# Merge gates as block products: seven products per 2 x 2 block instead of eight, in sweeps over pairs of column tiles, with the attention moved beside the branch gates

## The chip, the cores and the metric

The kernel runs on one NeuronCore of a Trainium2 chip. The metric is the device time of one execution in microseconds (us). The kernel before takes 2950.4 us in the median of 3 runs (2949.13 to 2953.23).

Engines in the profile: PE is TensorE (matmuls), PEld its weight loads, DVE VectorE, ACT ScalarE, POOL GpSimd, SP the engine that issues most DMAs. A product reads its operands from SBUF, sums in PSUM (8 banks), and an eviction by ScalarE or VectorE takes the sum out.

## The reference, cut to what matters

One layer of a decoder runs two token mixers on the same normalized input and merges them with gates. 1088 tokens (1024 of a prompt, 64 of 8 short samples), 2048 channels:

```python
h = rms_norm(x, norm_gain) * (1 + scale[:, None]) + shift[:, None]
u_a, z_a, q, k, v, z_b, g_lr, m_a, m_b = jnp.split(h @ w_in, SPLIT_POINTS, axis=-1)
a_y, sa_re, sa_im = s5_branch(u_a, ...)                       # state space
a_out = (a_y * jax.nn.silu(z_a)) @ w_a_out
b_y, s_gla = gla_branch(q, k, v, log_a, s0_gla, ...)          # gated linear attention
b_out = (b_y * jax.nn.silu(z_b)) @ w_b_out
merged = jax.nn.sigmoid(m_a) * a_out + jax.nn.sigmoid(m_b) * b_out
y = x + gate[:, None] * (merged @ w_out)
```

The merge gates m_a and m_b are 2048 columns each of `h @ w_in`, all in float32.

## The kernel before, in words

**Products.** All activations lie with channels on partitions: `h` is 16 tiles (k) of 128 channels x 1088 tokens. A float32 operand is split into a high and a low part, and a product is three passes: high weight x high activation, high x low, low x high (`mm3`, lines 63 to 71). `w_in` has 72 column tiles (j) of 128 columns. `product` (line 73) takes one column tile after the other: `wload` fetches its weights in four quarters of 128 x 512 (`wsplit`, line 46: SP's DMA into `wraw`, ScalarE writes the high part `whi`, VectorE the low part `wlo`; 6 buffers of each, so one tile and a half ahead). Then three chunks of tokens (320, 384, 384), for each 16 k x 3 passes = 48 matmuls into one PSUM bank `mm` of four, and an eviction: `evict_to` copies to DRAM, `evict_silu` multiplies with the sigmoid first.

With `kouter=True` two column tiles run side by side with k outside (`product_k`, line 91): the three sums of the first lie in `mm` banks, those of the second in three of the four `bg` banks that the work beside uses.

**Work beside the products.** `self.steps` is a generator that lays down small pieces of other work; `product` advances it after the k in `self.ticks` and after each chunk, and in the same way `self.gates`. In the stage of the merge gates it is the gated linear attention (`gla_run`, line 733): 20 units, 4 for the samples and 16 for the prompt (4 heads x 4 blocks of 256 tokens). A unit (`gla_unit`, line 756) is a chain over four engines. Head: gate product (L775), absolute value, exponential and logarithm on ScalarE (L778 to L780), difference and scans on VectorE (L784, L790). Seven levels (three for the samples), each: differences (L814), two exponentials (L815, L816), two products (L817, L818), small matmuls (L831, L840), a masked copy (L833). Tail: transposes (L872), copy (L874), matmuls with values and state (L932, L939, L940) and the state's update (L941), square (L945), sum on GpSimd (L946), mean over channels (L949), root (L132) and scaling. A unit's inputs are loaded while the unit before it runs.

**Order.** The program is laid down in this order: S5 beside the first products; tiles 16 to 31 (q, k, v); tiles 40 to 71 (the merge gates, to DRAM as `mas` and `mbs`) with the attention beside, `ticks` (4, 10); tiles 8 to 15 and 32 to 39 (branch gates `zas` and `zbs`) with `ada_gates` (the last columns of the conditioning product) beside; then both branches' outputs (`branch_a`, `merge`) and the output projection (`final`). The framework reorders what is laid down with a simulation of its own when the kernel is built, keeping all dependencies; what comes out is a fixed list for each engine, and each engine runs its list from the front. Buffers rotate: who allocates one waits for the last reader of what it held.

**Slots.** The pool of activations has 32 slots of 128 x 1088; in these stages `h`, in two parts, fills all of them.

## Time and profile before

| | |
|---|---|
| median of 3 runs | 2950.4 us |
| the profiled execution, its span | 2947.8 us |
| TensorE busy in the span | 2890.1 us (98%) |
| VectorE, ScalarE, GpSimd busy | 1344.5, 941.1, 263.4 us |
| granted TensorE clock, mean over the span | 0.994 |
| moved by DMA | 376.59 MB, 128 GB/s in the mean |

The page also has the chain of work that ended last: 67% of it are matmuls, 20% each on lines 69, 70 and 71, the three passes. In the 40 slices of the span TensorE is below nine tenths only in the first and in the last two.

How to read it: times are us from the span's start. A matmul's row shows from its start to its modelled end, and the next one starts before that, so what one costs is the distance of two starts. "Busy" of a group counts overlaps once. DMA share is the mean busy share of the 16 DMA engines. PEclk is the granted TensorE clock as a share of 2.4 GHz.

### The profile page before, as it was taken

The numbers are of one execution on the slowest core, as the hardware profiler recorded it, in microseconds if no ns is written. First come the engines' busy times: TensorE is split into PE (matmuls) and PEld (weight loads), VectorE is DVE, ScalarE is ACT, GpSimd is POOL, SyncE is SP. The second block draws the span as 40 slices with busy tenths as digits, with TensorE's granted clock in tenths as the row PEclk, the third lists the DMA queues.
The fourth block names the chain that finished last, engine by engine and source line by source line (L and its number), as shares of the span: only waits on it lengthen the run. The fifth ranks groups of instructions, "written<-read, shape, count | busy, mean of one in ns | idle before, by whom it ended". The sixth has DMA issues, their size and how long they took to land.

```text
span 2947.8 us, 49487 instructions
## 1 busy us (share of the span) xinstructions
PE 2890.1 (98%) x19584; PEld 2762.2 (94%) x19584; DVE 1344.5 (46%) x3424; ACT 941.1 (32%) x1735; POOL 263.4 (9%) x430
## 2 busy tenths in 40 slices
PE   7999999999999999999999999999999999999988
PEld 3799999999989999999999999999999999899988
DVE  3587778751234444444453111114662233556455
ACT  4222222222234434443443111422232111444434
POOL 0002122210000000000000000301010000203021
PEclk9999999999999999999999999999999999999999
DMA  9634444442232222222223344423274333555455
GB/s 377 242 117 122 120 128 117 128 123 75 85 126 100 84 83 72 85 80 77 81 86 105 98 146 132 115 76 102 97 231 136 112 114 116 191 164 181 145 173 168
DMA packets 221881, 376.59 MB, mean 128 GB/s; under 512 B 35153, under 2 KB 111729, under 8 KB 219473
## 3 DMA queue, kind: packets, MB, share of 16 engines
q1 hardware_dynamic: 159856, 256.26, 26.8%
q0 software_dynamic: 24720, 75.59, 8.4%
q10 hardware_dynamic: 37072, 41.59, 4.1%
q8 instruction: 154, 2.52, 0.3%
q14 instruction: 79, 0.64, 0.1%
HBM read 288.44 MB, written 76.51 MB: 124 GB/s over the span
## 4 chain that ended last, share of the span: by engine, by line
PE 67%; DMA 2%; DVE 1%; ACT 1%; issue 1%; POOL 0%; DVEq 0%; ACTq 0%; POOLq 0%
PE mm L71 20%; PE mm L69 20%; PE mm L70 20%; DMA wraw<-in_w_out_dram 1%; DMA bz<-zbs 1%; PE bg L831 1%; PE bg L69 1%; PE bg L71 1%; PE bg L70 1%; PE bg L201 1%; PE bg L939 0%; PE bg L940 0%; PE bg L932 0%; DMA mx<-mscr 0%; DVE wlo L56 0%
## 5 line engine op out<-in xcount | busy, mean ns | idle before, releaser
L69 PE MATMUL mm<-hh,whi 128*128 128x384 f32 (+1 forms) x3360 | 1101.3, 329 | 4.2 <-ACT hh L264 4.2
L71 PE MATMUL mm<-hh,wlo 128*128 128x384 f32 (+2 forms) x3360 | 1103.0, 329 | 0.0
L70 PE MATMUL mm<-hl,whi 128*128 128x384 f32 (+1 forms) x3360 | 1100.0, 328 | 2.4 <-DVE hl L266 2.4
L56 DVE TENSOR_TENSOR wlo<-wraw,whi 128x512 fp32r<-128x512 f32 x560 | 406.1, 729 | 634.7 <-ACT whi L54 627.2
L69 PEld LDWEIGHTS mm<-hh,whi 128*128 128x128 f32 x3360 | 630.5, 188 | 19.2 <-issue 10.0
L70 PEld LDWEIGHTS mm<-hl,whi 128*128 128x128 f32 x3360 | 630.6, 188 | 10.1 <-DVE hl L266 3.6
L71 PEld LDWEIGHTS mm<-hh,wlo 128*128 128x128 f32 x3360 | 630.5, 188 | 5.5 <-issue 2.8
L54 ACT ACTIVATE whi<-wraw 128x512 fp32r<-128x512 f32 x560 | 351.3, 630 | 771.8 <-PE mm L70 561.6
L69 PE MATMUL mm<-ahi,whi 128*128 128x384 f32 (+3 forms) x1656 | 542.0, 328 | 13.4 <-DVE y L1084 10.4
L71 PE MATMUL mm<-ahi,wlo 128*128 128x384 f32 (+3 forms) x1656 | 542.2, 328 | 2.9 <-DVE wlo L56 2.9
L70 PE MATMUL mm<-alo,whi 128*128 128x384 f32 (+3 forms) x1656 | 541.6, 327 | 0.0
L69 PEld LDWEIGHTS mm<-ahi,whi 128*128 128x128 f32 x1656 | 313.5, 189 | 17.1 <-issue 11.0
L71 PEld LDWEIGHTS mm<-ahi,wlo 128*128 128x128 f32 x1656 | 313.5, 189 | 4.8 <-DVE wlo L56 3.5
L70 PEld LDWEIGHTS mm<-alo,whi 128*128 128x128 f32 x1656 | 313.6, 189 | 1.1
L635 ACT ACTIVATE ev<-mm 128x384 f32<-128x384 f32 (+1 forms) x120 | 55.9, 466 | 237.4 <-PE mm L71 234.4
L1042 DVE TENSOR_TENSOR m<-m,mm 128x384 f32<-128x384 f32 (+1 forms) x96 | 50.5, 529 | 146.9 <-PE mm L71 146.9
L645 DVE TENSOR_TENSOR ev<-ev,mm 128x384 f32<-128x384 f32 (+1 forms) x45 | 23.8, 530 | 181.3 <-ACT ev L644 181.2
L946 POOL TENSOR_TENSOR on<-on 128x256 f32<-128x256 f32 (+1 forms) x20 | 13.1, 653 | 961.3 <-ACT on L945 961.3
L644 ACT ACTIVATE ev<-mm 128x384 f32<-128x384 f32 (+1 forms) x45 | 21.1, 468 | 176.5 <-PE mm L71 176.3
L1040 ACT ACTIVATE m<-m 128x1088 f32<-128x1088 f32 x32 | 35.6, 1113 | 119.3 <-DMA m<-mbs 91.3
L480 POOL DMA_DIRECT2D tm<-kd x128 | 65.0, 516 | 43.0 <-DMA kd<-kk 18.8
L991 POOL DMA_DIRECT2D yt<-y x64 | 34.1, 540 | 380.1 <-ACT m L207 259.6
(334 smaller groups left out, 2580.6 us busy)
## 6 DMA issues: line engine op xcount, KB each, us to landing
wraw<-in_w_in_dram SPq DMA_DIRECT2D x288, 256.0 KB
wraw<-in_w_out_dram SPq DMA_DIRECT2D x192, 256.0 KB
adaraw<-in_w_ada_dram SPq DMA_DIRECT2D x64, 512.0 KB
gateraw<-in_w_ada_dram SPq DMA_DIRECT2D x16, 1024.0 KB
x<-in_xT_dram SPq DMA_DIRECT2D x16, 544.0 KB
m<-mas POOLq DMA_DIRECT2D x16, 544.0 KB, 4.9
m<-mbs POOLq DMA_DIRECT2D x16, 544.0 KB, 5.0
mscr<-m POOLq DMA_DIRECT2D x16, 544.0 KB, 3.1
```

The lines of the kernel that those rows point to most:

```text
L54: nc.scalar.activation(hi, raw, AF.Copy)
L56: nc.vector.tensor_tensor(lo, raw, hi.bitcast(F32), ALU.subtract)
L69: nc.tensor.matmul(ps, hi[:, c], ah[:, sl], start=start, stop=False)
L70: nc.tensor.matmul(ps, hi[:, c], al[:, sl], start=False, stop=False)
L71: nc.tensor.matmul(ps, lo[:, c], ah[:, sl], start=False, stop=stop)
L201: self.nc.tensor.matmul(ps[i:i + 32, :256], self.c32[:, k, :], raw[:, (k - k0) * 256:(k - k0 + 1) * 256], start=k < 4, stop=k >= KT - 4, t ...
L480: nc.gpsimd.dma_start(tm[16 * s:16 * s + 16], kd[0:16, :, 16 * (7 - s):16 * (7 - s) + P])
L635: nc.scalar.activation(e[:, :n], ps[:, :n], AF.Copy, scale=scale)
L831: nc.tensor.matmul(o, gs, blk(gs, w)[:, :, m:w], start=True, stop=True, tile_position=(0, 32 * i))
L991: nc.gpsimd.dma_start(yv[r:r + 16], self.yscr[2 * i + uu][:, g, :].rearrange("(t h) c -> h t c", h=16))
L1040: nc.scalar.activation(st["m"], st["m"], AF.Sigmoid)
L1042: V.tensor_tensor(mm, mm, ps[:, :n], ALU.mult)
```

## The change

**The sums.** The weights of two neighbouring column tiles, halved over k (8 k tiles each), are a 2 x 2 block matrix a11, a12 (first tile), a21, a22 (second). The activations, halved over k and over tokens (2 x 544), are another: b11, b12, b21, b22. The product of two such matrices, eight block products, is made from seven by the scheme of Winograd and Strassen: the blocks are first added and subtracted (s1 to s4 on the left, t1 to t4 on the right), and the seven products are combined afterwards.

**Sweeps.** There are 16 pairs of column tiles, 8 for `mas` and 8 for `mbs`, each 8 a group. A sweep makes one of the seven products for the 8 pairs of a group; `SWEEPS` names left and right block. One product is 8 k x 2 half-width chunks of 272 tokens x 3 passes = 48 matmuls into two PSUM banks; `left` loads, adds, splits the left block (sums s1 and s2 go to DRAM and come back in the next sweep that uses them); the right block's 8 tiles are loaded during the sweep before into the other one of two sets. Partial results stay in 8 tiles (`pts`), finished quarters go to `mas` and `mbs`. All these tiles take the 32 slots that `h` had.

**Operands.** `blocks` writes the seven right blocks to DRAM (`opscr`), in steps beside the products 28 to 31.

**What moves.** The merge gates now come last before the branches. The branch gates (8 to 15, 32 to 39) come right behind 28 to 31, with the attention beside them, advanced after k 2, 6, 9, 13 and each chunk; `ada_gates` follows the attention in one generator (`behind`), which goes on in the sweeps after k 1, 3 and 5 of each product. The PSUM pool of the products is closed and opened anew on either side of the sweeps.

The diff without its changes of comments (a line of "..." marks what is left out):

```diff
+HT = T // 2
+NC = HT // 2
...
     def psum(self, main):
         if main:
-            return self.pmm.tile([P, 512], F32, tag="mm", name="mm")
+            return self.pmm.tile([P, 512], F32, tag="mm", name="mm", bufs=4)
...
+    SWEEPS = (("a11", "11"), ("a12", "21"), ("s1", "t1"), ("s2", "t2"), ("s3", "t3"), ("a22", "t4"), ("s4", "22"))
+
+    def blocks(self, h):
...
+            def split(name, k, v):
+                st = pp.tile([P, T], F32R, tag="st", name="st", bufs=3)
+                nc.scalar.activation(st[:, :HT], v, AF.Copy)
+                V.tensor_tensor(st[:, HT:], v, st[:, :HT].bitcast(F32), ALU.subtract)
+                nc.gpsimd.dma_start(self.opscr[name][k], st.bitcast(F32))
+            for k in range(8):
+                for name, (hi, lo), o in (("11", h[k], 0), ("21", h[8 + k], 0), ("22", h[8 + k], HT)):
+                    nc.gpsimd.dma_start(self.opscr[name][k][:, :HT], hi[:, o:o + HT].bitcast(F32))
+                    nc.gpsimd.dma_start(self.opscr[name][k][:, HT:], lo[:, o:o + HT].bitcast(F32))
+                x, y = (pp.tile([P, T], F32, tag=n, name=n, bufs=2) for n in "xy")
+                yield
+                V.tensor_tensor(x, h[k][0].bitcast(F32), h[k][1].bitcast(F32), ALU.add)
+                V.tensor_tensor(y, h[8 + k][0].bitcast(F32), h[8 + k][1].bitcast(F32), ALU.add)
+                b11, b12, b21, b22 = x[:, :HT], x[:, HT:], y[:, :HT], y[:, HT:]
+                V.tensor_tensor(b11, b12, b11, ALU.subtract)
+                split("t1", k, b11)
+                yield
...
+    def left(self, w, an, pair, q, scr, raws):
...
+        elif an == "s1":
+            x = both(blk(j2, 0), blk(j2, 1), ALU.add)
+            nc.gpsimd.dma_start(scr[0][:, q, :], x)
+        elif an == "s2":
+            x = both(load(scr[0][:, q, :]), blk(j1, 0), ALU.subtract)
+            nc.gpsimd.dma_start(scr[1][:, q, :], x)
...
+        hi = self.wp.tile([P, QK4], F32R, tag="whi", name="whi", bufs=6)
+        nc.scalar.activation(hi, x, AF.Copy)
+        lo = self.wp.tile([P, QK4], F32R, tag="wlo", name="wlo", bufs=6)
+        nc.vector.tensor_tensor(lo, x, hi.bitcast(F32), ALU.subtract)
+        return hi, lo
+
+    def sweeps(self, w, groups):
...
+        ops = [self.act(F32R, "op") for _ in range(16)]
+        sets = [ops[:8], ops[8:]]
+        right = lambda b, k, o: nc.sync.dma_start(o.bitcast(F32), self.opscr[b][k])
+        for k in range(8):
+            right("11", k, sets[0][k])
+        pts = [self.act(F32, "pt") for _ in range(8)]
+        rawt = [self.act(F32, "raw") for _ in range(4)]
+        fint = [self.act(F32, "fin") for _ in range(4)]
...
+                for i, (pair, dst) in enumerate(group):
+                    ps = self.pmm.tile([P, 2, 512], F32, tag="mm2", name="mm", bufs=2)
+                    for q in range(2):
+                        hi, lo = self.left(w, an, pair, q, self.wscr[i], raws)
+                        for k in range(4):
+                            c = slice(k * P, (k + 1) * P)
+                            b = B[4 * q + k]
+                            for m in range(2):
+                                o = ps[:, m, :NC]
+                                bh, bl = b[:, m * NC:(m + 1) * NC], b[:, HT + m * NC:HT + (m + 1) * NC]
+                                nc.tensor.matmul(o, hi[:, c], bh, start=q + k == 0, stop=False)
+                                nc.tensor.matmul(o, hi[:, c], bl, start=False, stop=False)
+                                nc.tensor.matmul(o, lo[:, c], bh, start=False, stop=q == 1 and k == 3)
+                            if 4 * q + k in self.ticks:
+                                next(self.steps, None)
+                    if nxt:
+                        right(nxt, i, N[i])
...
+    def behind(self):
...
+        yield from self.gla_run()
+        gla.close()
...
+        yield from self.ada_gates()
...
+        self.steps = self.blocks(h)
         self.product(w, range(28, 32), h, self.evict_v(24))
-        gla = ExitStack()
-        self.gla_pool(gla)
-        self.steps = self.gla_run()
-        self.ticks = (4, 10)
-        self.product(w, range(40, 56), h, self.evict_to(rows(40, self.mas)))
-        self.product(w, range(56, 72), h, self.evict_to(rows(56, self.mbs)))
         for _ in self.steps:
             pass
...
+        self.steps = self.behind()
+        self.ticks = (2, 6, 9, 13)
         self.product(w, range(8, 16), h, self.evict_silu(rows(8, self.zas)))
         ev = self.evict_silu(rows(32, self.zbs))
         self.product(w, range(32, 38), h, ev)
         self.product(w, [38, 39], h, ev, kouter=True)
-        for _ in self.gates:
+        self.pmmctx.close()
+        self.pmm = self.pool("pmm2", space=PSUM, ctx=self.pmmctx)
+        self.ticks = (1, 3, 5)
+        pairs = lambda j0, d: [((j0 + i, j0 + i + 1), (d[i], d[i + 1])) for i in range(0, 16, 2)]
+        self.sweeps(w, [pairs(40, self.mas), pairs(56, self.mbs)])
+        for _ in self.steps:
             pass
```

Two places of the built program show what the new order does; line numbers of the changed kernel are higher by 2 in the attention (L951 is the old L949, L777 the old L775, L803 the old L801, L833 the old L831).

TensorE before, where one unit of the prompt ends and the next begins, and where its first level's small matmuls come:

```order
L949 MATMUL bg<-on,ones_h 128x256
L775 MATMUL bg<-gr,wgu 128x256
L801 MATMUL bg<-q,k 32x32 x8
L71 MATMUL mm<-hh,wlo 128x320
L69 MATMUL mm<-hh,whi 128x320
L70 MATMUL mm<-hl,whi 128x320
...
L70 MATMUL mm<-hl,whi 128x384
L831 MATMUL bg<-g 32x16 x16
L71 MATMUL mm<-hh,wlo 128x384
```

From one L775 to the next stand 197 to 218 product matmuls, through all 20 units.

TensorE now, behind the sixth unit of the prompt, beside the branch gates:

```order
L951 MATMUL bg<-on,ones_h 128x256
L777 MATMUL bg<-gr,wgu 128x256
L803 MATMUL bg<-q,k 32x32 x8
L833 MATMUL bg<-g 32x16 x40
L842 MATMUL bg<-g 32x32 x4
L842 MATMUL bg<-g 64x64 x2
L874 MATMUL bg<-ident,kd 128x128 x2
L934 MATMUL bg<-v,kT 128x256 x2
L941 MATMUL bg<-scp,v 128x128
L942 MATMUL bg<-q,St_10028 128x128
```

Up to here 198 to 217 product matmuls stand between one L777 and the next. From this place on there is none: this unit and six more follow each other whole, with the start of an eighth, 502 matmuls in a row. The last rows of it, and what comes behind (column tile 39, whose sums are in `bg` banks; tile 38 stands ahead of the stretch, and the sweeps behind tile 39):

```order
L777 MATMUL bg<-gr,wgu 128x256
L803 MATMUL bg<-q,k 32x32 x8
L833 MATMUL bg<-g 32x16 x16
L71 MATMUL bg<-hh,whi 128x320
L72 MATMUL bg<-hl,whi 128x320
L73 MATMUL bg<-hh,wlo 128x320
L71 MATMUL bg<-hh,whi 128x384
```

ScalarE before, in a unit beside merge gates, whose evictions are copies (L635):

```order
L816 ACTIVATE d<-d 128x4x32
L635 ACTIVATE ev<-mm 128x320
L815 ACTIVATE d<-d 128x2x64
L816 ACTIVATE d<-d 128x2x64
L636 DMA mbs_158<-ev 128x320
L874 ACTIVATE kT<-bg 128x256
```

ScalarE now, in a unit beside branch gates, whose evictions are sigmoids (L646):

```order
L818 ACTIVATE d<-d 128x16x8
L56 ACTIVATE whi<-wraw 128x512
L646 ACT_TABLE_LOAD
L646 ACTIVATE ev<-mm 128x384
L648 DMA zas_129<-ev 128x384
L817 ACT_TABLE_LOAD
L817 ACTIVATE d<-d 128x8x16
L818 ACTIVATE d<-d 128x8x16
```

Each change between sigmoid and exponential now has a table load ahead of it; in the whole program there are 119 such loads, where there were 98.

## Rows read from the trace of the kernel before

**Rows 1.** The page, busy time of each engine, share of the span, instructions.

```profile
PE 2890.1 (98%) x19584; PEld 2762.2 (94%) x19584; DVE 1344.5 (46%) x3424; ACT 941.1 (32%) x1735; POOL 263.4 (9%) x430
```

**Rows 2.** Windows (stretch: length, busy of each engine, clock, DMA share, GB/s).

```profile
660.00:760.00 100.00, 99.38 (x618) 98.71 (x618) 11.26 (x17) 23.40 (x53) 0.00 (x0) 1.00 0.26 80
760.00:1650.00 890.00, 888.69 (x6954) 846.85 (x6953) 372.43 (x1089) 349.91 (x743) 13.06 (x20) 1.00 0.27 89
```

**Rows 3.** Timeline, TensorE (start, duration, line, operands): 384, 320, 256 columns, first and last.

```profile
899.47 0.33 PE L69 MATMUL mm<-hh,whi 128*128 128x384 f32 x1
...
901.38 0.33 PE L71 MATMUL mm<-hh,wlo 128*128 128x384 f32 x1
...
217.61 0.31 PE L69 MATMUL mm<-hh,whi 128*128 128x320 f32 x1
...
219.07 0.31 PE L70 MATMUL mm<-hl,whi 128*128 128x320 f32 x1
...
2889.23 0.28 PE L70 MATMUL mm<-alo,whi 128*128 128x256 f32 x1
...
2891.51 0.28 PE L71 MATMUL mm<-ahi,wlo 128*128 128x256 f32 x1
```

**Rows 4.** Timeline, all engines: the head of one unit of the prompt.

```profile
1311.68 0.59 PE L949 MATMUL bg<-on,ones_h 128*128 128x256 f32 x2
1311.92 0.47 PE L775 MATMUL bg<-gr,wgu 96*128 96x256 f32 x1
...
1312.31 0.47 ACT L132 ACTIVATE t<-bg,eps 128x256 f32<-128x256 f32 x1 [3.33 <-PE bg L949]
1312.68 0.40 ACT L774 ACTIVATE gr<-gt 96x256 fp32r<-96x256 f32 x1
...
1316.72 0.46 ACT L778 ACTIVATE t<-bg 128x256 f32<-128x256 f32 x1
...
1320.77 0.42 DVE L784 TENSOR_TENSOR t<-b,t 128x256 f32<-128x256 f32 x1 [2.73 <-ACT t L780]
...
1321.90 0.73 DVE L790 TENSOR_TENSOR_SCAN b<-one,t 128x128 f32<-128x128 f32 x2
```

**Rows 5.** Groups by form (line, operation, count, busy us, mean ns): levels, table loads.

```profile
L814 DVE TENSOR_TENSOR d<-b 128x256 f32<-128x256 f32 x112 | 43.5, 418 | 0.5
L817 DVE TENSOR_TENSOR g<-d,k 128x128 f32<-128x128 f32 x112 | 31.8, 284 | 0.0
L833 DVE COPY_PREDICATED scd<-masks,bg 128x32 f32<-128x32 uint8 x80 | 16.2, 202 | 35.1 <-PE bg L831 35.1
...
L779 ACT ACT_TABLE_LOAD x19 | 24.4, 1283 | 0.3
```

**Rows 6.** Timeline, all engines: the tail of the same unit.

```profile
1338.23 0.44 PE L872 MATMUL bg<-ident,kd 128*128 128x128 f32 x2
...
1338.70 0.38 ACT L874 ACTIVATE kT<-bg 128x256 f32<-128x256 f32 x1 [7.07 <-PE bg L872]
...
1342.33 1.02 PE L932 MATMUL bg<-v,kT 128*128 128x256 f32 x4
...
1344.29 0.48 DVE L941 SCALAR_TENSOR_TENSOR St<-St,eb,bg 128x256 f32<-128x256 f32 x1 [0.58 <-PE bg L940]
...
1348.13 0.38 PE L940 MATMUL bg<-q,St 128*128 128x128 f32 x2
...
1349.73 0.73 POOL L946 TENSOR_TENSOR on<-on 128x256 f32<-128x256 f32 x1 [41.24 <-ACT on L945]
```

**Rows 7.** Windows near the end: a stall, weight loads alone, stores alone.

```profile
2852.00:2856.00 4.00, 2.51 (x12) 2.54 (x13) 3.06 (x5) 1.96 (x4) 4.00 (x7) 0.50 0.63 200
2860.00:2864.00 4.00, 1.43 (x12) 1.23 (x11) 0.00 (x0) 0.41 (x1) 0.00 (x0) 1.00 1.03 399
2940.00:2944.00 4.00, 0.00 (x0) 0.00 (x0) 2.04 (x4) 0.00 (x0) 0.91 (x1) 0.50 1.02 338
```

More of the change, by code (lines that the diff above doesn't have):

```diff
@@ L34, in __init__ @@
         self.ctx, self.tc, self.nc, self.a = ctx, tc, tc.nc, a
-        self.steps = self.gates = iter(())
+        self.steps = iter(())
         self.ticks = (7,)
@@ L88, in product @@
                 next(self.steps, None)
-                next(self.gates, None)
     def product_k(self, w, js, act, nk, evict):
@@ L150, in setup @@
         self.dp = self.pool("scratch", space=DRAM)
[L151 removed]
         self.pbg = self.pool("pbg", bufs=4, space=PSUM)
+        self.pmmctx = ExitStack()
+        self.pmm = self.pool("pmm", space=PSUM, ctx=self.pmmctx)
         cp = self.cp
@@ L1055, in merge @@
             self.product(a["w_b_out"], [j], bb, eb)
+    SWEEPS = (("a11", "11"), ("a12", "21"), ("s1", "t1"), ("s2", "t2"), ("s3", "t3"), ("a22", "t4"), ("s4", "22"))
+    def blocks(self, h):
+        nc = self.nc
+        V = nc.vector
+        with ExitStack() as ctx:
+            pp = self.pool("blocks", ctx=ctx)
+            def split(name, k, v):
[15 more added lines that the diff above has]
+                yield
+                V.tensor_tensor(b12, b22, b12, ALU.subtract)
+                split("t3", k, b12)
+                V.tensor_tensor(b11, b22, b11, ALU.subtract)
+                split("t2", k, b11)
+                yield
+                V.tensor_tensor(b21, b11, b21, ALU.subtract)
+                split("t4", k, b21)
@@ L1058, in final @@
+    def behind(self):
+        gla = ExitStack()
+        self.gla_pool(gla)
+        yield from self.gla_run()
+        gla.close()
+        gates = ExitStack()
+        self.gp2 = self.pool("gates", ctx=gates)
+        yield from self.ada_gates()
+        gates.close()
     def final(self):
@@ L1149, in run @@
         self.oscr = [dram([P, 2, T], f"o{i}") for i in range(4)]
+        self.opscr = {n: [dram([P, T], f"op{n}_{k}") for k in range(8)] for n in ("11", "21", "t1", "t2", "t3", "t4", "22")}
+        self.wscr = [[dram([P, 2, QK4], f"ws{p}_{i}") for i in range(2)] for p in range(8)]
         self.ada_inputs()
@@ L1201, in run @@
         self.product(w, [38, 39], h, ev, kouter=True)
-        for _ in self.gates:
-            pass
-        gates.close()
+        self.pmmctx.close()
[4 more added lines that the diff above has]
+        for _ in self.steps:
+            pass
+        self.pmmctx.close()
+        self.pmm = self.pool("pmm3", space=PSUM)
         self.p2ctx = ExitStack()
```

69 lines of the change are left out of this document (64 added, 5 removed).

## The prediction

> **What bounds the kernel now.** I read the page's totals first, then the stretches by stage, then single matmuls. TensorE is busy 98% of the span [rows 1], and in the stage that the change rebuilds (the 32 column tiles 40 to 71 of `w_in`, with the attention beside them) it is busy 888.69 of 890 us at the full clock, while VectorE has 372, ScalarE 350 and the DMA engines 0.27 of their time [rows 2]. So there the time is the sum of what TensorE must stream, and every instruction of another engine is hidden. What one matmul costs is read from start to start, not from its duration (durations overlap): 11 steps of 384 columns take 1.91 us, or 0.1736 each, 10 steps of 320 take 1.46 (0.146), and 19 steps of 256 take 2.28 (0.120) [rows 3]. A shorter matmul is thus dearer per column: 0.452, 0.456 and 0.469 ns.
>
> **The products.** Removed: 32 tiles x 16 k x 3 passes x (0.146 + 2 x 0.1736) = 757.6 us. Added: 16 pairs x 7 products x 8 k x 2 halves x 3 passes = 5376 matmuls of 272 columns, which no row shows. Between 256 and 320 columns on a line it is 0.120 + 16/64 x 0.026 = 0.1265 us, so 680 us: 77.5 us less, not the eighth (95 us) that the column count gives. Bounds: at 0.120, 112 us less; at 0.146, 27 us more. The pages bear on this price: the Trainium skill ("TensorE: Matmul & The Clock Gate", section "Wait — 56ns, not 53.3ns?") has the step as columns / 2.4 GHz plus 2.5 ns. By that rule the sweeps take 623 us, some 57 less than I count. The trace does not agree: the rule gives 109 ns for 256 columns where [rows 3] have 120.
>
> **The attention, which is the decisive part.** It does not vanish: the stage's 890 us less 757.6 leave 132 us of TensorE for 20 units, 6.6 each (4 units of samples, 16 of the prompt). Before, each unit lies spread among 197 to 218 product matmuls, one stride after another. Now the generator is called five times per chunk instead of three, but the order of the built program (section on the change) still has some 216 product matmuls per unit, so that at the end of column tile 38 the generator is far ahead of what has been placed: the sixth prompt unit closes and then seven whole units and the beginning of an eighth stand on TensorE with no product matmul between them, 502 matmuls in a row. Only then come the 144 matmuls of tile 39, whose sums lie in the banks that the attention uses, and behind these the sweeps, whose operands take the slots that tile 39 still reads. TensorE runs its instructions in their order, so in this stretch it waits for one unit's chain after the other.
>
> How long is a bare unit? I follow the chain of one unit through the trace, leaving out waits for product matmuls. Head [rows 4]: the mean square (0.59), root (0.47), next unit's gate copy (0.40), gate product (0.47): 1.93. From the start of Abs (1316.72) to the subtraction (1320.77), with two table loads inside, 4.05. Subtraction 0.42, scans 0.73, the first differences 0.42 [rows 5], the first exponentials some 0.5: 2.07. Levels: seven, each with differences 0.42, two products of 0.28 [rows 5] that start closer than they last, and a masked copy of 0.20: 1.1 each, 7.7 in all. Tail [rows 6]: last scores and transposes (0.44 each), copy 0.38, the value and output products until the state's update starts (1342.33 to 1344.29: 1.96), the update 0.48, from the second group to GpSimd's sum (1348.13 to 1349.73: 1.60), the sum 0.73: 6.0. Together 21.8 us. Below: if of each level only the differences (0.42) show, 14.1 + 2.9 = 17. Above: with TensorE busy only a third of such a stretch, its clock may fall; after the stall near the end of this kernel the granted clock stands at 0.50 (the 1.2 GHz level), with 12 matmuls in 2.51 us [rows 7]. TensorE's own pieces of the chain are 4.8 us, so 26.6 with all of them doubled. I take 24, between 21.8 and 26.6.
>
> Seven units of 24 and the eighth up to its second level (8) are 176 us. Of this 7.3 x 6.6 = 48 are the matmuls that had to be run anyway: +128 us (bounds 79 and 147). The Trainium skill (same page, section "Step-by-step: what each phase is for") says that only weight loads are pulled ahead and that matmuls stay in program order. No run here shows that apart; if tile 39's matmuls could be pulled forward, 144 x 0.1645 = 24 us of the gap would be filled.
>
> **The smaller parts.** *Feeding the sweeps.* Sweeps three and four move per product 4 loads and 2 stores of 256 KB and one operand tile of 544 KB, 2.13 MB in 48 x 0.1265 = 6.07 us, or 351 GB/s; the others 177 to 309. Full DMA engines moved 399 GB/s of such weight loads and 338 of stores [rows 7]. At 399 it is hidden; at 338 each of these 32 products takes 0.23 us more (7 us). On top, the 16 loads of the branch gates (16.8 MB, 42 to 50 us of all engines) now fall into the first three sweeps: half of them uncovered would be 25. I take 8, range 0 to 33. *The operand blocks* (`blocks`), beside tiles 28 to 31: 31.2 MB of stores, 78 to 92 us of full engines, in a stage of 95 us that already uses 0.26 of them [rows 2]. So it runs at the limit; its copies queue on GpSimd, and VectorE and ScalarE wait there for the third staging slot back, with the weight parts behind them. 0 to 18, I take 4, since VectorE has 88 of 100 us free there and the stores run on after the stage. *Entry and exit of the sweeps*: the first left blocks use slots of h[12] and h[13], which tile 39 reads until 3/4 of its way, and the last operand set is free for the first branch only when the last product ends: 6 (0 to 14). *Table loads*: beside sigmoid evictions the exponentials of a unit need three or four loads more, 1.28 us each [rows 5], 38 us of ScalarE over ten units; 22 to 26 product matmuls stand between two groups of a unit and hide them. I take 3; uncovered, up to 20. The sweeps' evictions (8 half-width sums per pair) lie beside 42 us of matmuls and cost nothing while two pairs of banks alternate.
>
> Sum: -77.5 + 128 + 8 + 4 + 6 + 3 = +71.5, on the profiled span 2947.8: 3019.3. The median of the runs, 2950.4, is 2.6 above that span: **3022 us**.
>
> **Rivals.** *The stretch is filled or short (faster).* If a bare unit took 13 us, because ScalarE starts the next unit's gate while the last is being normalized, the stretch would cost 7 x 13 + 8 - 48 = 51, and with 15 for the small parts the kernel ends at 2950.4 - 77.5 + 51 + 15 = 2939. It decides from a unit below 14.5 us. Against it: gate copy and Abs stand behind the root on ScalarE, and the root needs the unit's last product. 5%, with 2% for a draw around it. *The sweeps are bound by transfers*: all small terms at their upper ends (33 + 18 + 14 + 20) and the stretch at 140: 2950.4 - 77.5 + 140 + 85 = 3098. For it, mixed reads and writes above 340 GB/s are shown nowhere; against it, the mean over the seven products of a pair is 277 (11.8 MB in 42.5 us). 19%. *The matmul does not get shorter below 320 columns*: 785 instead of 680, 3127; the 256-column rows speak against it. 3%. *The step loses its fixed part*: 0.120 us for 256 columns is 13 ns above 256 / 2.4 GHz; were that gone in the new loop, whose weight tile serves two matmuls in a row, 5376 x 13 ns = 70 us less, 2952. Against it: all three sizes of [rows 3] have it, also where two passes share their weights. 3%. The Trainium skill's rule above (same page, section "Wait — 56ns, not 53.3ns?") would end there at 2965. *The order is not what decides* (the products on the chip cover the units after all) would need TensorE to run them out of order: it is inside the first rival's 5%.
>
> **How the numbers follow.** Forecast 68%, 2985 to 3060 by the bounds of the unit; transfers 19%, long matmuls 3%, short step 3%, faster or equal 7%. A range of 2972 to 3088 leaves out the faster cases and the worst of the transfers. 0.2%, some 6 us, is about what can be told from no change here: faster 5%, same 2%, slower 93%.
>
> **What would show it.** TensorE: 160 to 185 us between the end of the evictions of tile 38 and the first matmul of tile 39, busy for a third, at the 0.50 clock, with waits for VectorE and ScalarE; the distance of two gate products (L777) there 21 to 27 us. In the sweeps steps of 0.126 us and busy TensorE, at a DMA share of 0.8 to 1.0. The prediction is wrong if units in that stretch follow at under 15 us, if TensorE waits for `whi` or `wlo` for more than 40 us in the sweeps, or if steps of 272 columns are nearer 0.115 or 0.146.

## The result, and the profile after

The changed kernel took 3109.5 us (median of 4 runs, 3106.1 to 3111.3) beside 2949.9 for the kernel before: ratio 1.0535, 95% interval 1.0520 to 1.0549. I had said slower, at 3022 us, in a range that ended at 3088. The direction and the place of the main loss were right; of the 160 us that came I had less than half. The profiled execution has a span of 3104.4 us, 156.6 more than before.

The page of the changed kernel: busy time of each engine, then the span in 40 slices with the granted clock and the DMA share. It answers to [rows 1].

```profile
PE 2859.1 (92%) x20352; PEld 2716.8 (88%) x20352; DVE 1627.7 (52%) x3856; ACT 1020.0 (33%) x1804; POOL 377.3 (12%) x638
...
PE   7899999999999996338889999999999999999988
...
PEclk9999999999999998558999999999999999999999
DMA  9854444457332221115599976897346333544555
```

TensorE is busy 31 us less than before and the span is 157 longer, so it stands still for some 190 us more (245 instead of 58). This shows in slices 16 to 21: first a hole with idle DMA engines and a low clock, then a shallower one in which the DMA engines are half busy at first and then full. By stages (length, busy of each engine, clock, DMA share, GB/s), which answers to [rows 2]:

```profile
660.00:776.00 116.00, 115.27 (x713) 114.31 (x713) 76.53 (x111) 48.03 (x96) 17.04 (x32) 1.00 0.73 244
776.00:1198.00 422.00, 414.20 (x3098) 387.94 (x3097) 190.19 (x564) 202.13 (x377) 4.96 (x9) 1.00 0.29 92
1198.00:1403.00 205.00, 81.05 (x1015) 65.15 (x1013) 114.11 (x360) 98.30 (x204) 5.79 (x8) 0.60 0.12 38
...
1430.00:1660.00 230.00, 201.32 (x1817) 179.63 (x1816) 97.89 (x228) 72.67 (x131) 31.75 (x58) 0.93 0.76 264
1660.00:1760.00 100.00, 88.27 (x675) 85.79 (x674) 56.62 (x88) 27.98 (x35) 26.81 (x50) 0.98 1.00 317
1760.00:1940.00 180.00, 180.00 (x1448) 180.00 (x1448) 67.00 (x102) 42.05 (x68) 13.48 (x25) 1.00 0.73 255
```

The third row is the attention alone, the fourth the first three sweeps, the fifth the fourth sweep and most of the fifth one. In the last row the sweeps run as they were meant to, without a gap. There 19 steps of 272 columns take 2.36 us, 0.1242 each (timeline of TensorE; the prediction worked out 0.1265 from [rows 3]):

```profile
1850.81 0.29 PE L1176 MATMUL mm<-op,whi 128*128 128x272 f32 x1
...
1853.17 0.29 PE L1177 MATMUL mm<-op,wlo 128*128 128x272 f32 x1
```

The bare units, in the timeline of TensorE and ScalarE from one gate product (L777) to the next (in [rows 4 and 6] the same work lay beside products):

```profile
1228.10 2.07 PE L934 MATMUL bg<-v,kT 128*128 128x256 f32 x4 [0.47 <-ACT kT L876]
...
1235.91 0.47 PE L777 MATMUL bg<-gr,wgu 96*128 96x256 f32 x1
1236.30 0.47 ACT L133 ACTIVATE t<-bg,eps 128x256 f32<-128x256 f32 x1 [0.29 <-PE bg L951]
1236.67 0.40 ACT L776 ACTIVATE gr<-gt 96x256 fp32r<-96x256 f32 x1
1240.30 0.47 ACT L780 ACTIVATE t<-bg 128x256 f32<-128x256 f32 x1 [3.22 <-DVE rsn L142]
1240.79 1.28 ACT L781 ACT_TABLE_LOAD   x1
...
1261.89 0.77 PE L777 MATMUL bg<-gr,wgu 96*128 96x256 f32 x1
```

This unit took 25.98 us; the seven periods from 1207.91 to 1393.0 average 26.4 (the first 28.0, the six behind it 26.2). The value products take 2.07 us where [rows 6] have 1.02: half the clock. And Abs (L780), which I had put right behind the gate's copy, waits 3.2 us for the last Newton step of the unit before. The waits of TensorE, then of ScalarE in the stretch (us in total, times, longest):

```profile
PE bg L833 <- DVE g L820: 86.2, 21, 12.0
```

```profile
ACT t L780 <- DVE rsn L142: 26.4, 8, 3.5
```

Where the 156.6 us went, against the terms of the sum:

| Step of the prediction | forecast | measured | from |
|---|---|---|---|
| products | -77.5 | -90 | 5376 x 0.1242 - 757.6 |
| bare units | +128 | +149 | 1207.7 to 1405.0, less the 48 of work in it |
| stores of operand blocks | +4 | +15 | last transposes of v at 763.1 before, 778.0 after |
| table loads, waits beside the tiles of z | +3 | +8 | 422 - 414.2 |
| sweeps: feeding, entry, exit | +14 | +71 | 1430.4 to 2208.3 = 777.9, less 668 of products, some 18 of units, 21 of gates |

They add up to 153. From `branch_a` on the kernels agree (897.4 and 896.1 us).

### The profile page after: what moved, and what is told of

Its sections match the earlier page's. It is cut to its first block, busy times and chain, and to the rows that moved or that the text cites. A ratio compares the mean times of both kernels' runs of the same rounds, so it can differ in the third digit from the quotient of the medians.

```text
span 3104.4 us, 52753 instructions
## 1 busy us (share of the span) xinstructions
PE 2859.1 (92%) x20352; PEld 2716.8 (88%) x20352; DVE 1627.7 (52%) x3856; ACT 1020.0 (33%) x1804; POOL 377.3 (12%) x638
## 4 chain that ended last, share of the span: by engine, by line
PE 59%; DMA 10%; DVE 7%; issue 6%; ACT 4%; POOL 1%; SPq 0%; ACTq 0%; DVEq 0%; POOLq 0%
PE mm L73 12%; PE mm L71 12%; PE mm L72 12%; PE mm L1175 5%; PE mm L1177 5%; PE mm L1176 5%; DMA raw<-in_w_in_dram 3%; DMA wraw<-in_w_in_dram 2%; DMA op<-opt 1%; DMA wraw<-in_w_out_dram 1%; DMA raw<-ws 1%; ACT L781 1%; DMA bz<-zbs 1%; DVE rsn L134 1%; DVE wlo L58 1%
## 5 line engine op out<-in xcount | busy, mean ns | idle before, releaser
L71 PE MATMUL mm<-hh,whi 128*128 128x384 f32 (+1 forms) x1824 | 596.2, 328 | 8.5 <-ACT hh L266 8.5
L72 PE MATMUL mm<-hl,whi 128*128 128x384 f32 (+2 forms) x1824 | 599.6, 329 | 3.1 <-DVE hl L268 2.8
L73 PE MATMUL mm<-hh,wlo 128*128 128x384 f32 (+3 forms) x1824 | 599.9, 330 | 0.0
L71 PE MATMUL mm<-ahi,whi 128*128 128x384 f32 (+3 forms) x1656 | 542.7, 328 | 11.2 <-DVE y L1246 8.6
L1175 PE MATMUL mm<-op,whi 128*128 128x272 f32 x1792 | 521.8, 291 | 19.7 <-ACT whi L1127 10.3
L1177 PE MATMUL mm<-op,wlo 128*128 128x272 f32 x1792 | 521.4, 291 | 3.0 <-DVE wlo L1129 3.0
L1176 PE MATMUL mm<-op,whi 128*128 128x272 f32 x1792 | 517.0, 289 | 0.0
L1175 PEld LDWEIGHTS mm<-op,whi 128*128 128x128 f32 x1792 | 341.8, 191 | 27.3 <-ACT whi L1127 17.8
L71 PEld LDWEIGHTS mm<-hh,whi 128*128 128x128 f32 x1824 | 342.5, 188 | 16.0 <-ACT hh L266 11.0
L72 PEld LDWEIGHTS mm<-hl,whi 128*128 128x128 f32 x1824 | 342.7, 188 | 11.8 <-DVE hl L268 4.7
L73 PEld LDWEIGHTS mm<-hh,wlo 128*128 128x128 f32 x1824 | 343.0, 188 | 4.6 <-issue 2.6
L1177 PEld LDWEIGHTS mm<-op,wlo 128*128 128x128 f32 x1792 | 340.8, 190 | 6.4 <-DVE wlo L1129 4.3
L1176 PEld LDWEIGHTS mm<-op,whi 128*128 128x128 f32 x1792 | 339.8, 190 | 0.1
```

What stands on the lines that cost most here:

```text
L71: nc.tensor.matmul(ps, hi[:, c], ah[:, sl], start=start, stop=False)
L72: nc.tensor.matmul(ps, hi[:, c], al[:, sl], start=False, stop=False)
L73: nc.tensor.matmul(ps, lo[:, c], ah[:, sl], start=False, stop=stop)
L1175: nc.tensor.matmul(o, hi[:, c], bh, start=q + k == 0, stop=False)
L1176: nc.tensor.matmul(o, hi[:, c], bl, start=False, stop=False)
L1177: nc.tensor.matmul(o, lo[:, c], bh, start=False, stop=q == 1 and k == 3)
```

## The experiments

The kernels are told by their labels. The times of the sweeps below are from the timeline of TensorE, from the first of 384 matmuls to the first of the next 384; five columns of 14 sweeps in the order in which they run. The last column has the units of the attention that start in the sweeps, and whether the gates' products lie there.

| Kernel | 1 to 3 | 4, 5 | 6 to 8 | 9 to 11 | 12 to 14 | units in them, gates |
|---|---|---|---|---|---|---|
| 272 columns x 0.1242 | 143.1 | 95.4 | 143.1 | 143.1 | 143.1 | |
| changed | 224.8 | 111.9 | 143.4 | 151.7 | 146.2 | 2, gates |
| e4, gates first | 198.2 | 105.7 | 147.9 | 148.4 | 146.6 | 4 |
| e9, late y | 224.9 | 95.6 | 144.4 | 158.3 | 155.4 | 2, gates |
| e13, gates' loads out | 210.3 | 108.1 | 143.6 | 149.6 | 147.3 | 2, gates |
| e6 | 193.8 | 119.4 | 171.8 | 169.4 | 144.8 | 11 |
| e14, y in rows | 191.9 | 120.9 | 171.4 | 145.5 | 150.7 | 11 |

**e1_steps.** Fewer calls of the attention beside the tiles of z:

```diff
-        self.ticks = (2, 6, 9, 13)
+        self.ticks = (4, 10)
```

> The attention is called three times per chunk of columns beside the tiles of z_a and z_b instead of five, so that by the built order 10 units stand there, 8 among the sweeps' products and the last two bare behind the fifth sweep, with the gates behind them. Theory A (the stretch of bare units costs some 150 us over the work in it, the gates' loads some 45, the transfers of the sweeps some 25): 776 for the front + 380 for tiles of z + 20 units of 6.6 + 668 of sweeps + 20 of gates + 896 behind = 2872, + 25 for transfers, 35 for two bare units, 45 for the gates = 2977 in the profile, 2955 to 3010 as a time. Theory B (the sweeps are bound by their own transfers, and units that now stand beside them lie in their shadow or make it worse; the stretch is not what decides): not below 3060. The distance of two gate products (L777) goes from 26 us to over 30, the sum of TensorE's waits for VectorE's g (L820) from 98 us to under 30 by theory A.

3020.5 us (ratio 1.0243, 1.0226 to 1.026): 89 less than the changed kernel. Theory B falls; theory A gave 2955 to 3010, 10 too low. The bare row was not gone but shorter, and stood where the built order had it, in the sixth sweep, with two whole units, the end of another and the gates behind them. Beside products the gate products are 38 to 58 us apart, as expected; the waits for g fell only to 50 us. The window of that sweep, and TensorE's waits from tile 8 to the last sweep:

```profile
1568.00:1728.00 160.00, 103.50 (x1037) 82.00 (x1036) 70.47 (x198) 47.42 (x101) 10.62 (x19) 0.75 0.55 194
```

```profile
PE bg L833 <- DVE g L820: 50.2, 25, 10.7
PE bg L203 <- DMA gateraw<-in_w_ada_dram: 12.9, 2, 12.4
```

**e2_banks.** Tile 39 out of the attention's banks:

```diff
-        self.product(w, range(32, 38), h, ev)
-        self.product(w, [38, 39], h, ev, kouter=True)
+        self.product(w, range(32, 40), h, ev)
```

> Column tiles 38 and 39 are computed one after the other in the banks of the main products, as tiles 32 to 37 are, instead of side by side with tile 39 in banks of the attention. By the built order the bare row of units is still there (574 matmuls instead of 502), but behind the second pair of the sweeps' first product. Theory A (the generator runs ahead because it is called too often; where tile 39 stands is not the cause): within 30 us of the changed kernel, 3080 to 3140. Theory C (tile 39's banks hold the products up until the units have let go of them): the stretch falls apart, the time falls by over 100, to under 3010.

3111.9 us (1.0554, 1.053 to 1.0578). Theory C falls: the first sweep takes 314 us instead of 73, with eight units in it, 25 to 31 us apart. Where tile 39's sums lie is not what makes the bare row; that the number of calls decides how long it is, e1 shows.

**e3_scratch.** Another buffer for the root's scratch:

```diff
-        rs, rt = new("rsn")[:, :n], new("t1")[:, :n]
+        rs, rt = new("rsn")[:, :n], new("kd")[:, :n]
```

> The root's scratch tile takes the buffer of kd instead of that of t1, in which the next unit's Abs writes, so that Abs need not wait for the Newton step of the unit before. Theory A (this wait, 3.2 to 3.5 us in the trace of the changed kernel, is in the chain of every bare unit, and I had not counted it): the period of the bare units falls from 26.4 to about 23, and with seven units instead of eight in the row by the built order the time falls by 20 to 50, to 3060 to 3090. Rival (the chain of a bare unit goes through VectorE and TensorE alone, Abs is early enough anyway): period 26 and at most 20 less for the shorter row, over 3088.

3080.2 us (1.0439, 1.0423 to 1.0454), 29 less. The bare units are 23.8 to 25.2 apart, 24.3 in the mean of six. Abs now starts behind the root (timeline of ScalarE):

```profile
1242.06 0.47 ACT L133 ACTIVATE kd<-bg,eps 128x256 f32<-128x256 f32 x1 [0.29 <-PE bg L951]
1242.44 0.47 ACT L780 ACTIVATE t<-bg 128x256 f32<-128x256 f32 x1
```

So the shared scratch buffer is some 2 us of each bare unit (26.2 in the six periods of the changed kernel behind the first, 24.3 here), and without it a unit takes the 24 us of my working. In seven units that is some 13 of the 29 us; the rest goes with the one unit fewer that stands bare by the built order (24 us less its own 6.6, an estimate).

**e4_gates_first.** The two blocks of `behind` change places:

```diff
+        gates = ExitStack()
+        self.gp2 = self.pool("gates", ctx=gates)
+        yield from self.ada_gates()
+        gates.close()
         gla = ExitStack()
         self.gla_pool(gla)
         yield from self.gla_run()
         gla.close()
...
```

> The chunks of the conditioning product for the gates (16 loads of 1 MB) come in front of the attention, beside the first tiles of z_a, instead of behind it beside the first three sweeps; by the built order seven bare units instead of eight stand in the row, and four units instead of two beside the sweeps. Theory A (in the first three sweeps, which took 225 us for 143 of products, some 45 are due to the gates' loads, the rest to matmuls of units and gates): these three sweeps take 170 to 190 with four units, and the time falls by 40 to 90, to 3020 to 3070. Theory B (the sweeps are bound by their own transfers there): they still take over 210, and the time falls by less than 30.

3079.1 us (1.0442, 1.0426 to 1.0457), 30 less: under theory A's 40 to 90, at the edge of theory B's 30. The first three sweeps take 198 with four units, outside both.

**e5_four.** The edits of e1, e3 and e4, and the 48 stores of parts of h held until tile 28: they go to one DRAM tile whose space is free only when a tiny transfer out of the `blocks` pool has been written to it.

```diff
+            z = pp.tile([1, 8], F32, name="z")
+            V.memset(z, 0.0)
+            nc.sync.dma_start(self.hold[0, 0:1, 0:8], z)
+            big = self.dp.tile([24, P, T], F32, name="opbig", tag="hold")
...
```

> The changed kernel with four edits together: three calls of the attention per chunk instead of five beside the tiles of z, the gates' chunks in front of the attention, the root's scratch in kd's buffer, and the 48 stores of the operand blocks that are parts of h held back until tile 28. By the built order no unit stands bare: 9 units are beside the tiles of z, 11 among the sweeps' products. Theory A: front 762 + tiles of z 380 + 20 units of 6.6 + gates 20 + sweeps 668 + 896 behind = 2858, and some 35 of stalls at the sweeps' entry and in those of sums: 2893 in the profile, 2880 to 2925 as a time, faster than the kernel before by 1 to 2%. Rival: eleven units among the sweeps hold up the weight parts on VectorE and ScalarE, and the sweeps are bound by transfers on top; they lose over 90 beside their own work, and the time is 2950 or more.

2948.9 us (0.9997, 0.9986 to 1.0008): no difference to the kernel before. No unit is bare, but the sweeps take 800 us for 668 of products and 73 of eleven units: 59 of stalls, not 35, and they begin at 1244 us, 23 later than in my sum. Neither theory's number holds: theory A is 24 us off its range, and the rival's 90 of loss are not there either.

**e6_early_stores.** The same without the holding back.

> As the four edits together, but the 48 stores of parts of h stay where the change has them, at the front of GpSimd's queue between 52 and 165 us. Theory A (they take transfers from the conditioning product's loads there: tile stage 10 us late, as the changed kernel showed): 8 to 18 us slower than with the four edits, with the products of w_glr starting 10 us later than before. Rival (these 10 us are of the draw of the profiled execution): the same within 4 us.

2947.8 us (0.9994, 0.9985 to 1.0004), the same as e5. So the rival's number holds, but not its reason. Theory A's 10 us at the front are there: the product with w_glr, ahead of tiles 16 to 31, starts at 312.4 instead of 302.3 (299.2 before). Held back, however, the stores cost most of that later: the last transposes of v, at the end of tiles 28 to 31, come at 780.7 here and at 777.6 in e5. There the 13.4 MB came in bursts, 21 of the 48 stores between 630 and 647 us, and TensorE waited 6.8 us for an eviction of v.

**e7_plain.** The same without sweeps and blocks (`product` over tiles 40 to 71, as before).

> As the four edits together, but the 32 tiles of the merge gates' columns are plain products as before, without the sweeps and without the operand blocks: what is left of the change is the order of the stages, the gates in front and the scratch tile. Theory A: 757.6 of products instead of 668 and no stalls of sweeps: within 12 us of the kernel before, 2938 to 2960, so that the seven products for eight are worth 40 to 60 net. Rival (the order alone costs something, as units beside sigmoid evictions load tables): over 2965.

2958.1 us (1.003, 1.0019 to 1.0042). The new order alone costs 9 us. Against this the seven products for eight, 90 us of TensorE, were worth 9 us in e5, not 40 to 60.

**e8_one_block.** In `left`, every weight part from one load:

```diff
-        elif an == "s1":
-            x = both(blk(j2, 0), blk(j2, 1), ALU.add)
-            nc.gpsimd.dma_start(scr[0][:, q, :], x)
...
+            x = blk(j1, 1 if an == "s4" else 0)
+            both(x, x, ALU.add)
```

> As the four edits together, but it leaves out the second block of each sum or difference on the left, and the stores and reloads of sums: every weight part of the sweeps is made of one loaded block (added to itself, so that VectorE has the same additions). Matmuls, evictions and operands stay. Theory A (the stalls of some 25 us in the sweeps of sums, third, fourth, tenth and eleventh, are the transfers' rate): these stalls go, 15 to 35 us less than with the four edits. Rival (they come from VectorE, whose additions and evictions queue before the weight parts): within 8 us of the four edits.

2927.7 us (0.9931, 0.9916 to 0.9945): 21 less than e5, within theory A's range. But sweeps 3 and 4, which were to gain most, gained 5 us together, and 9 to 11, with no unit beside them, gained 10 and still lost 19. Something else moved there: the DMA list of e5 in sweeps 9 to 11 (transfer, queue, count, size, us to landing) has it.

```profile
ws<-raw POOLq DMA_DIRECT2D x25, 256.0 KB, 6.1
...
yt<-y POOLq DMA_DIRECT2D x40, 68.0 KB, 6.6
```

These are the loads of y for the first branch (`gelu_y`). Before, they lay beside the tiles of z, from 1860 to 2014 us, and landed in 3.6 us each. They start when the space of the attention's or the gates' pool comes free, in the changed kernel in sweeps 3 to 5 (56 of the 64).

**e9_late_y, e10_four_y.** That space is kept by a copy that is laid down in the twelfth sweep (e10: the four edits with it):

```diff
                     elif r == 4:
+                        if g == 1 and i == 0:
+                            V.tensor_copy(self.keep, x[:, 0:1])
...
+        self.keep = self.gp2.tile([P, 1], F32, name="keep")
         yield from self.ada_gates()
-        gates.close()
...
```

> The changed kernel, with one edit: the space that the gates leave is kept until the twelfth sweep (a copy of one column into a tile of theirs), so that the 64 loads of y for the first branch, which take that space, come in the last three sweeps instead of the third to fifth, in front of whose stores they stand in GpSimd's queue. Theory D (these loads, in rows of 544 bytes, and not the sweeps' own loads and stores, are what holds up the sweeps of sums): the fourth and fifth sweep go from 60.6 and 51.3 us to under 51 and 49, the time falls by 10 to 25, to 3085 to 3100. Theory A (2.13 MB per product of the sums are themselves too much): the fourth sweep stays over 57, the time within 6 us.

3103.3 us (1.052, 1.0506 to 1.0534), 6 less, not the 10 to 25 of theory D. The loads of y start at 2005.8 us, already in the eleventh sweep. Theory D holds for the place: the fourth and fifth sweep take 47.8 us each, at the full clock and a DMA share of 0.91. The two kernels' windows of these sweeps, the changed one first:

```profile
1655.00:1767.00 112.00, 100.27 (x771) 97.79 (x770) 60.65 (x94) 29.88 (x38) 29.17 (x55) 0.98 1.00 314
```

```profile
1651.00:1747.00 96.00, 96.00 (x773) 96.00 (x773) 57.27 (x89) 20.24 (x33) 9.21 (x17) 1.00 0.91 318
```

But sweeps 11 to 14 give 16.5 back (214.2 us instead of 197.7). A move of the loads within full sweeps gains nothing.

> The four edits together, and y held until the twelfth sweep. There the y loads stand in sweeps 9 to 11, which take 59.1, 54.9 and 57.4 us with no unit beside them. Theory D: these three go to under 50 each, and the time falls by 18 to 30, to 2919 to 2931. Theory A: they stay over 53, the time within 8 us of the four edits' 2949. If y then comes too late, the first matmul of w_glu waits, and up to 15 of the gain goes.

2940.8 us (0.998, 0.9968 to 0.9991), 8 less than e5 instead of 18 to 30: sweeps 9 and 10 take 48.6 and 49.9, the eleventh, where y now stands, 59.7, the last three 154.2 instead of 146.0.

**e11_four_mid, e12_six.** The 48 stores behind the last u, from 300 us on; and this with the late y.

> The four edits together, but the 48 stores of parts of h are issued behind the last u, from about 300 us on, where the DMA engines are half free, instead of beside tiles 28 to 31. Theory A (13.4 MB more either at the front or beside tiles 28 to 31 cost 10 to 15 us by the transfers, wherever the engines are full): the last transposes of v move from 778 to 763 to 768 us, and the time falls by 8 to 16, to 2933 to 2941. Rival (the operand blocks' cost is that of their copies and sums on ScalarE and VectorE beside tiles 28 to 31): within 5 us of the four edits.

> All of it: the four edits, the stores of parts of h from 300 us on, and y held until the twelfth sweep. If both theories hold, 18 to 30 and 8 to 16 less than 2949: 2903 to 2923, faster than the kernel before by 0.9 to 1.6%. If only one of them holds, 2925 to 2940; if neither, 2949.

2947.8 (0.9999, 0.9991 to 1.0008) and 2944.2 us (0.9984, 0.9975 to 0.9992). The time of e11 is the rival's, but it does not show the rival's reason. The stores found free engines but stood in GpSimd's queue among the loads of the S5 tables, and TensorE waited 11.2 us for S5's rotations between 300 and 580 us (3.1 in e5): the first transposes of v come at 580.1 us (561.3 in e5), the last at 786.5.

**e13_gate_once.** One load for all gates' chunks, on the changed kernel:

```diff
-                raw = self.gp2.tile([P, 2048], F32, tag="raw", name="gateraw", bufs=3)
-                nc.sync.dma_start(raw, a["w_ada"][j][:, k * 256:(k + 8) * 256])
+                if j == 16 and k == 0:
+                    raw = self.gp2.tile([P, 2048], F32, tag="raw", name="gateraw", bufs=3)
+                    nc.sync.dma_start(raw, a["w_ada"][j][:, k * 256:(k + 8) * 256])
```

> The changed kernel; it leaves out 15 of the 16 loads of the gates' chunks (all their matmuls read the first one). Matmuls, transposes and their places stay. Theory A' (with the gates in front, the first three sweeps lost some 22 us less; that is what the loads cost beside the sweeps): the first three sweeps go from 225 to 198 to 208 us, the time falls by 15 to 28, to 3081 to 3095. Rival (it is the gates' matmuls and the units' rests that hold the sweeps up, not the loads): within 6 us of the changed kernel.

3086.7 us (1.0472, 1.0457 to 1.0486), 23 less. The first three sweeps take 210 us, 14.5 less than with all loads and 2 over the range. What is left of the gates is one wait (TensorE, the first three sweeps of this kernel):

```profile
PE bg L203 <- DMA gateraw<-in_w_ada_dram: 12.8, 1, 12.8
```

It is the first load, whose space the attention's last unit still held, while its matmuls already stood in TensorE's order.

**e14_y_rows.** e6, with y stored as the branch reads it:

```diff
-        self.bgq.dma_start(self.yscr[u], y)
+        for t in range(8):
+            self.bgq.dma_start(self.yscr[u // 2][64 * (u % 2):64 * (u % 2) + 64, t, :].rearrange("(g h) c -> h g c", h=16), y[16 * t:16 * t + 16])
...
+        nc.gpsimd.dma_start(y.rearrange("p (s c) -> p s c", s=8), self.yscr[i])
```

> The four edits without the held-back stores, so as e6; y is stored by the S5 part in the order in which the first branch reads it (128 stores of 34 KB, rows of 544 bytes, there), so that the branch reads it in 8 loads of whole rows of 4352 bytes. Theory D (64 loads in rows of 544 bytes fill the engines in sweeps 9 to 11, with 200 to 270 GB/s at a share of 0.9): these sweeps (56.2, 54.3, 59.0 in e6) go to 155 us or less together, the time falls by 8 to 20, to 2928 to 2940. Rival (the bytes count, or the place in GpSimd's queue): the three stay over 163, the time within 5 us of e6's 2948.

2928.1 us (0.9933, 0.992 to 0.9947): 20 less than e6, and faster than the kernel before. Sweeps 9 to 11 take 145.5 us instead of 169.4. Windows of these sweeps in e5 (as e6, but with the stores of parts of h held back) and in e14:

```profile
1727.00:1899.00 172.00, 155.24 (x1160) 153.86 (x1159) 74.55 (x116) 45.61 (x57) 42.99 (x80) 0.92 0.90 284
```

```profile
1732.00:1879.00 147.00, 145.33 (x1165) 144.83 (x1164) 75.02 (x116) 42.24 (x55) 23.29 (x43) 1.00 0.92 324
```

A like share of the engines moved 324 GB/s instead of 284. In all, the bytes of y are the same; in this window fewer of them start (3 loads of 544 KB against 40 of 68 KB), since four more start just ahead of it. Whether it was the rows, the 16 partitions of each load or the 64 places in GpSimd's queue, this run does not tell apart; the last section shows that the engines themselves spend longer on y's small loads, which places in a queue alone do not explain.

**e15_paced, e16_both.** Each step of `blocks` releases its own six stores (eight DRAM tiles instead of one); and this with y's rows.

```diff
+                nc.gpsimd.dma_start(self.hold[k][0, 0:1, 0:8], x[0:1, 0:8])
+                big = self.dp.tile([3, P, T], F32, name=f"opb{k}", tag=f"hold{k}")
...
```

> As the four edits, but each of the eight steps of the operand blocks releases its own six stores of parts of h, so that they neither stand at the front (e6) nor come at once at the start of tile 28 (e5). Theory A (13.4 MB cost time only where they come in a burst beside full engines or behind an eviction's store): w_glr starts at 298 to 303 as before, the last transposes of v come at 764 to 771 instead of 778 to 781, and the time falls by 6 to 14, to 2935 to 2943. Rival (the stage of tiles 28 to 31 cannot take 31 MB in its 100 us at all; what is not lost in front is lost there): over 775, the time within 5 us of 2949.

2937.6 us (0.9963, 0.995 to 0.9976), 10 less than e6, with w_glr at 299.6 and the last transposes of v at 769.0 us: what the stores cost depended on when they came. Some 8 us of the operand blocks remain (760.6 in e7, without blocks), and the rival, that this stage cannot take the 31 MB at all, is out.

> The paced stores and y's rows together with the other three edits. If both theories hold, 2920 to 2932, faster than the kernel before by 0.6 to 1.0%; if one, 2932 to 2942; if none, 2945 to 2952.

2929.4 us (0.9928, 0.9913 to 0.9943): within the range for both, but no better than e14. The last transposes come 8.7 us earlier than in e14, and the sweeps take 6.6 us more (1246.1 to 2033.0 and 1248.7 to 2029.0). Of the versions that compute the whole layer e14 and e16 are the fastest, 0.7% under the kernel before; e15, e10 and e12 are 0.4, 0.2 and 0.2% under it.

## Why the prediction was wrong in size

**The step that failed is the feeding of the sweeps**, with its neighbours at entry and exit: 14 forecast with 47 as upper bound, 71 measured. I took it as a rate, the sweeps' own 351 GB/s against 399 and 338 [rows 7]. The own transfers were nearly as cheap as I said: with y out of the way the fourth sweep, one of the two that I held for the hardest, runs at 47.8 us, as the fifth does (e9). My own sign for this step did not show it either: TensorE waited 13.3 us for `whi` and `wlo` in the sweeps, not 40. What cost were transfers of others that the change moved in beside them. The gates' 16 loads I had counted, but as bytes: 14.5 us are theirs (e13), and 13 more are the first load's late start, a wait and no rate (12.8 of it still there in e13). The loads of y I had not seen at all: they belong to code that the diff does not touch, but take space that the change sets free at another time. They cost 16.5 us in the changed kernel (e9). Of the other 27 us, 8.6 are sweeps 9 to 11 and 3.1 the last three; the rest lies in the first three, with the rests of two units at a clock of 0.93, and was not taken apart. The waits of TensorE for these parts in the sweeps of the changed kernel, 1430 to 2209 us (us in total, times, longest):

```profile
PE bg L203 <- DMA gateraw<-in_w_ada_dram: 18.4, 4, 13.1
PE mm L1175 <- ACT whi L1127: 10.3, 7, 2.8
PE mm L1177 <- DVE wlo L1129: 3.0, 5, 1.1
```

**The bare units** were the decisive part, as forecast: 149 us (128; bounds 79 to 147), just over the bound. Place, mechanism, idle TensorE and low clock came as described; the row of 502 matmuls took 197 us, over the 160 to 185 that I had given as its sign. A unit was 26.4 us, not 24: some 2 are the root's scratch buffer (e3), 13 of the 21 us. In [rows 4] it does not show, since there an eviction and a weight part stood on ScalarE ahead of Abs. But it stood in the groups by form of the kernel before, where I read the durations and not the idle time behind them (count, busy, mean ns, idle before and its releaser):

```profile
L778 ACT ACTIVATE t<-bg 128x256 f32<-128x256 f32 x16 | 7.4, 466 | 23.9 <-DVE rsn L141 23.9
```

The granted clock was 0.58 to 0.60 in the mean over the stretch, near the 1.2 GHz level (0.50), which my upper bound had allowed for. e2 rules out the rival that tile 39's banks are the cause, e1 shows that the number of calls is.

**The products** are worth more than forecast: -90 instead of -77.5, since 272 columns take 0.1242 us, nearer to the 256-column step than a line gives. The two rivals on the step are out. By the Trainium skill's rule ("TensorE: Matmul & The Clock Gate", section "Wait — 56ns, not 53.3ns?") the step is an estimated 0.1158; this row does not agree, by 8 ns.

**The operand blocks** cost 15 us, not 4, within the 0 to 18. The place was wrong: I had all stores beside tiles 28 to 31, where TensorE in fact was busy 115.3 of 116 us. But 48 of them read only h, and stand first in GpSimd's order, from 52 us on, where the DMA engines are busy for 0.91 of the first 180 us in the changed kernel and w_glr comes 10.9 us later; in e15, without them there, it comes at 299.6 again. I had read the order at the places of the diff and not from the start of the queue.

**Table loads**, with the waits beside the tiles of z, took 8 us in place of 3, within the 20. TensorE waits there for g alone, nine times, and each time 3 to 5 us after a sigmoid's table load (L646) on ScalarE. So the loads may be in these waits; no run takes that apart.

The rival "transfer-bound sweeps" (3098) came nearest in its number. Its mechanism was only half right. In the fourth and fifth sweep all transfers together filled the engines (share 1.00), and the sweeps' own alone did not (0.91 in e9). In the first three, where most was lost, the engines were busy 0.76 of the time.

## What to carry to other kernels

A stage that is rebuilt changes when its neighbours' memory comes free, and so when transfers start that no line of the diff names: follow every DMA queue of the new order from its first row, and ask of each pool that closes who takes the space. Time that a change frees on the engine that bounds is not gained by itself: here 90 us on TensorE became 9 (e5 against e7). 17 of the others are the stores of the operand blocks (last transposes of v, e5 against e7) and 59 are stalls in the sweeps; the layout of an unrelated load gave 20 back (e14), and what else stalls there was not taken apart. Work that is hidden beside products has its own chain; before it is laid bare, look for buffers that two of its rounds share.

## What the runs showed of the hardware that I had not expected

Transfers of the same bytes differed in what they took of the engines. At full share, the changed kernel's sweeps 4 and 5 moved 314 GB/s with 35 loads of y (2.4 MB in pieces of 68 KB) among them, and e9's moved 318 at 0.91, which is 350 at full share. At 350 the other 32.8 MB of that window take 94 of the 112 us, so those 2.4 MB cost some 18 (an estimate from the two windows). The DMA queues of the two windows say where these 18 us are (packets, MB, share of 16 engines; q0 has GpSimd's transfers, the loads of y and all stores, q1 the loads of SP). The changed kernel, 112 us:

```profile
q1 hardware_dynamic: 11944, 27.03, 75.8%
q0 software_dynamic: 2854, 8.03, 23.5%
```

e9, 96 us:

```profile
q1 hardware_dynamic: 11202, 25.37, 77.2%
q0 software_dynamic: 1480, 4.99, 13.1%
```

In e9 the stores moved at 397 GB/s of full engines (4.99 MB in 0.131 of 96 us). At that rate 5.6 of the 8.03 MB of the changed kernel take 14.1 of 26.3 us, so the 2.4 MB of y took 12 us themselves, some 200 GB/s. The other 6 us are SP's loads, which ran at 318 GB/s of full engines beside y instead of 342. (All are estimates from these rows.) That y is dear by itself shows in the kernel before, where the engines were a third busy and q0 had nothing but loads of y (1860 to 2014 us): 4.25 MB in 0.134 of 154 us, 206 GB/s.

```profile
q0 software_dynamic: 1947, 4.25, 13.4%
```

The Trainium skill ("DMA: Bandwidth & Descriptors", section "Measured (HBM→SBUF, 128 partitions, SWDGE, issued from GpSimd)") has 138 GB/s for a transfer of 64 KB over 128 partitions. The loads of y are of 68 KB over 16 partitions and took the engines at 200 to 206; no run here shows the page's case.
